# Spreading a side norm over more groups of a feed-forward, moving transposes a part ahead, and four copies a layer to VectorE

## The chip, the cores and the metric

The kernel runs on one core of a Trainium2 chip. The time is the device time of one execution in microseconds (us), as the median of several runs. The engines are TensorE (PE for its matmuls, PEld for its weight loads), VectorE (DVE), ScalarE (ACT), GpSimd (POOL) and the sync engine (SP), whose queue issues the loads of weights.

## The reference

Two layers of a decoder, on 256 tokens of width 1024 and a memory of 256 rows:

```python
mem_n = layer_norm(mem, mem_ln_g, mem_ln_b)
for l in range(DEPTH):                       # DEPTH = 2
    h = layer_norm(ALPHA * x + 0.5 * swiglu(x, ffn1_w_gu, ffn1_w_down), ln_g[0], ln_b[0])
    (dn_q, dn_k, dn_v, dn_b, dn_a, dn_z, sw_q, sw_k, sw_v, xa_q, gates) = split(h @ w_in)
    o_dn = deltanet_branch(...)              # gated delta rule
    o_sw = sliding_window_attention(...)     # 8 heads, window 128, with sinks
    o_xa = memory_cross_attention(xa_q, mem_n, w_mem_kv)
    merged = sum over n of sigmoid(gates[n]) * (branch[n] @ w_branch[n])
    h = layer_norm(ALPHA * h + merged @ w_out, ln_g[1], ln_b[1])
    x = layer_norm(ALPHA * h + 0.5 * swiglu(h, ffn2_w_gu, ffn2_w_down), ln_g[2], ln_b[2])
```

Everything is float32. The norm of the memory (`mem_n`) is computed once and used in both layers.

## The kernel before, in words

**Three matmuls for one product.** Each float32 operand is split into a rounded high half and the rest. `split` (lines 120 and 121) does it: a cast on ScalarE for the high half, then a subtraction on VectorE for the low one. `mm3` multiplies high by high, high by low and low by high. In the profile both instructions of every split, and so those of the weights, stand under line 121, and all matmuls under line 130.

**The stream of weights.** The weights lie in one long stream in the order of use. `unit` (line 104) takes the next 128x1024 block of 512 KB: a load on SP's queue into one of three `raw` buffers (line 115), a cast into one of five `whi` buffers on ScalarE, a subtraction into one of five `wlo` buffers on VectorE. A `raw` buffer can be loaded again when its subtraction is done. Engines and queues run their instructions in the order in which the planner wrote them; the instructions of `unit` are given a priority 300 places ahead of their place in the program (`AHEAD`). `load` (line 76) is for all other loads; those keep the program's order among themselves and share SP's queue with the weights.

**A feed-forward** (`Ffn`) has 11 groups of 256 gate and 256 up columns. A group takes 4 units; per unit TensorE does 2 rows of k for two row blocks of 128 tokens, 12 matmuls of 512 columns. The two banks of a group (of four `acc` banks in PSUM that go round) are read by `out` (line 338): SiLU on ScalarE (line 344), a product on VectorE (line 345) into a tile `t`, a 32x32 transpose on VectorE (line 348), four DMAs on POOL's queue to memory (`tr`, line 354) and one back (`pt`, line 355). `settle` splits what comes back into the high and low halves of the hidden tile. `rest` (line 366) does groups 1 to 10 and then the down projection, 22 units of one k each, into four banks: the first two units are run for row block 0 and then for row block 1, the others for both blocks in turn. So the down projection needs the banks of groups 9 and 10 right behind group 10.

**Side work between groups.** `rest` takes a table `mid`: behind `out` of group i it calls the steps 2i and 2i+1, and what these put on VectorE is queued behind the last product of that group. In layer 0 the table holds the norm of the memory (`memory_T`, line 429) and some loads: step 5 loads small parameters (`small`), 7 and 9 the two row blocks of the stream (`xres`), 8 loads the memory as rows (`vecs`), 10 is `rows_`, 13 loads the transposed memory (`halves_`), 15 and 17 are `half(0)` and `half(1)`, 19 is `keep`.

- `rows_` (line 453) takes mean and variance of each row with bn_stats (459, 460), then the reciprocal root by `rsqrt` (254 to 261), 11 small VectorE instructions, once for each row block; a VectorE transpose (465), four POOL DMAs to memory (467) and one back (469) that spreads means and roots over all partitions, into the tile `gB`.
- `half(q)` (line 476) subtracts the mean (479) and multiplies by the root (480) on 128x1024 of the transposed memory, scales and shifts on ScalarE (483), and splits the result.
- `keep` writes the four halves to memory (441, POOL's queue) for layer 1, which reads them back.

The transposed memory goes into the same two buffers (`pp`) as its rows, so its loads wait for the statistics.

**The mixers** (`mixers`, line 500) keep TensorE's order as written (`pinned`). `weave` runs a generator of matmul parts and calls extra steps behind the part with a given number. Attention weights are turned on TensorE into PSUM (`at`, two banks) by `x_turn` and `w_turn`, and copied out by ScalarE (lines 687 and 741), one copy for each block of 128 keys (`kb`). The values of the window branch go into tiles `oS` (tags u10 and u11), those of the memory branch into `oX` (u6 and u7), whose last reader is `branch(0, oX)`.

The last branch, `branch(2, oT)` (line 960), has four parts of 12 matmuls: row block 0 columns 0 and 1, row block 1 columns 0 and 1. Behind each part VectorE multiplies by the gate (973) and adds to the merged stream `mg` (976). `merge_turn(tb, q)` (line 1011) transposes 128x512 of `mg` on TensorE (line 133) and splits it into `mgT`, the operand of the output projection. `merge_turn(0, 0)` stands behind part 3, `(0, 1)` behind part 4, and `(1, 0)` and `(1, 1)` in `between`, that is after the first two units of the output projection for row block 0. Those two units read only the columns that `merge_turn(0, 0)` makes.

## Time and profile before

| what | before |
|---|---|
| time, median of 3 runs | 1291.05 us (1289.76 to 1291.07) |
| time of the profiled execution | 1291.24 us |
| its span, first to last instruction | 1289.5 us |
| PE busy | 1264.1 us, 98% of the span |
| DVE busy | 855.4 us, 66% |
| ACT busy | 661.3 us, 51% |
| POOL busy | 199.8 us, 15% |
| DMA | 263.50 MB moved, 204 GB/s in the mean |
| granted TensorE clock, mean | 0.995 |

A row of the timeline gives the start and duration in us, the engine, the line, the operation, what it writes and reads, and in brackets how long the engine had been idle before it and what ended that. A row of the groups has the count, the busy us and the mean duration in ns, then the idle us. A row of the waits says which instruction waited for which, with the total us, how often, and the longest. A row of the stage view has a stretch, then for each engine its busy us and instructions, the granted TensorE clock as a share of full speed, and the DMA traffic. TensorE's instructions are pipelined, so a row's duration is longer than the step to the next one.

### The profile page before, as it was taken

The page shows a single profiled execution, that of the slowest core. Times are in us where ns is not written, and L with a number is a line of the kernel's source. Part 1 is how long each engine was busy: PE and PEld are TensorE (multiplying, and loading weights), DVE is VectorE, ACT ScalarE, POOL GpSimd, SP SyncE. Part 2 cuts the span into 40 slices and gives each one's busy share as a digit, 9 for nine tenths or more (in the row PEclk, how much of TensorE's full clock was granted, in tenths as well). Part 3 has the DMA queues.
Part 4 walks back from the last instruction along what each step waited for, and adds up shares of the span by engine and source line. Part 5 has one row for each costly group of instructions (what it writes and reads, how often), then busy time and mean ns, then how long its engine had stood idle before and what let it go on. Part 6 is the DMA issues. An engine that isn't in the chain of part 4 may idle for free.

```text
span 1289.5 us, 18743 instructions
## 1 busy us (share of the span) xinstructions
PE 1264.1 (98%) x6944; PEld 1075.7 (83%) x6944; DVE 855.4 (66%) x1273; ACT 661.3 (51%) x979; POOL 199.8 (15%) x361
## 2 busy tenths in 40 slices
PE   8999899999999999999999999999999999999997
PEld 6887688999878788888888888899988787888886
DVE  5676557797556786665576665758867378666555
ACT  5545444666574545444445444446556554454441
POOL 1232100102411002221012220000023100022200
PEclk9999899999999999999999999999999999999999
DMA  8887774654543648887768777656454256487762
GB/s 271 303 277 255 247 239 125 219 169 136 155 154 122 203 138 272 246 244 229 245 211 262 245 242 213 198 167 209 165 151 146 98 178 231 139 262 241 243 217 107
DMA packets 78075, 263.50 MB, mean 204 GB/s; under 512 B 11968, under 2 KB 13120, under 8 KB 77984
## 3 DMA queue, kind: packets, MB, share of 16 engines
q1 hardware_dynamic: 66320, 232.53, 56.0%
q0 software_dynamic: 11664, 29.77, 8.1%
q8 instruction: 54, 0.88, 0.3%
q14 instruction: 37, 0.30, 0.1%
HBM read 247.45 MB, written 14.81 MB: 203 GB/s over the span
## 4 chain that ended last, share of the span: by engine, by line
PE 75%; DMA 10%; DVE 7%; ACT 4%; issue 3%; POOL 0%; SPq 0%; DVEq 0%; ACTq 0%; POOLq 0%
PE acc L130 65%; DMA raw<-in_wst_dram 9%; PE at L130 3%; PE sm L130 3%; DVE wlo L121 3%; ACT whi L121 2%; PE sm L133 1%; PE acc L326 1%; PE acc L323 1%; PE acc L324 1%; DMA tr<-t 1%; DVE h L286 1%; DVE bnst L272 1%; DVE h L404 1%; DVE u L121 1%
## 5 line engine op out<-in xcount | busy, mean ns | idle before, releaser
L121 DVE TENSOR_TENSOR wlo<-raw,whi 128x1024 fp32r<-128x1024 f32 (+2 forms) x403 | 484.9, 1209 | 329.3 <-ACT whi L121 328.0
L121 ACT CAST whi<-raw 128x1024 fp32r<-128x1024 f32 (+2 forms) x403 | 414.1, 1033 | 444.4 <-PE acc L130 234.7
L130 PE MATMUL acc<-whi,hT 128*128 128x512 f32 (+1 forms) x1824 | 563.6, 387 | 5.0 <-ACT whi L121 5.0
L130 PEld LDWEIGHTS acc<-whi,hT 128*128 128x128 f32 x1824 | 341.3, 188 | 72.9 <-ACT whi L121 5.0
L130 PE MATMUL acc<-wlo,hT 128*128 128x512 f32 (+1 forms) x912 | 351.3, 385 | 0.0
L130 PE MATMUL acc<-whi,u 128*128 128x512 f32 x784 | 252.2, 395 | 6.6 <-DVE t L345 6.6
L130 PEld LDWEIGHTS acc<-wlo,hT 128*128 128x128 f32 x912 | 171.9, 189 | 32.9 <-DVE wlo L121 0.7
L130 PEld LDWEIGHTS acc<-whi,u 128*128 128x128 f32 x784 | 148.4, 189 | 39.9 <-DVE t L345 5.5
L130 PE MATMUL acc<-wlo,u 128*128 128x512 f32 x392 | 153.9, 393 | 0.0
L354 POOL DMA_DIRECT2D tr<-t x176 | 96.2, 553 | 353.3 <-DVE t L348 337.0
L130 PE MATMUL acc<-hT,whi 128*128 128x256 f32 x672 | 122.3, 284 | 0.0
L130 PEld LDWEIGHTS acc<-hT,whi 128*128 128x128 f32 x672 | 104.7, 192 | 0.0
L130 PE MATMUL acc<-hT,wlo 128*128 128x256 f32 x336 | 95.1, 283 | 0.0
L130 PEld LDWEIGHTS acc<-wlo,u 128*128 128x128 f32 x392 | 74.3, 190 | 14.9
L130 PEld LDWEIGHTS acc<-hT,wlo 128*128 128x128 f32 x336 | 64.4, 192 | 0.0
L355 POOL DMA_DIRECT2D pt<-tr x44 | 25.0, 568 | 182.7 <-DMA tr<-t 124.5
L344 ACT ACTIVATE t<-acc 128x256 f32<-128x256 f32 x88 | 32.8, 378 | 23.0 <-PE acc L130 23.0
L345 DVE TENSOR_TENSOR t<-t,acc 128x256 f32<-128x256 f32 x88 | 36.2, 416 | 6.7 <-ACT t L344 4.4
L121 DVE TENSOR_TENSOR u<-pt,u 128x512 fp32r<-128x512 f32 x44 | 29.0, 659 | 10.3 <-ACT u L121 10.3
L529 DVE SCALAR_TENSOR_TENSOR t<-acc,cw,t 128x255 f32<-128x255 f32 (+2 forms) x72 | 34.4, 478 | 0.9
L130 PE MATMUL acc<-whi,w 128*128 128x512 f32 x96 | 31.7, 401 | 2.5 <-DVE w L121 2.5
L121 ACT CAST u<-pt 128x512 fp32r<-128x512 f32 x44 | 26.9, 612 | 12.5 <-DMA pt<-tr 12.5
(248 smaller groups left out, 1188.0 us busy)
## 6 DMA issues: line engine op xcount, KB each, us to landing
raw<-in_wst_dram SPq DMA_DIRECT2D x409, 512.0 KB, 4.3
tr<-t POOLq DMA_DIRECT2D x176, 64.0 KB, 3.8
pt<-tr POOLq DMA_DIRECT2D x44, 256.0 KB, 4.6
raw<-in_wst_dram SPq DMA_DIRECT2D x16, 324.0 KB, 2.8
gB<-in_lnp_dram SPq DMA_DIRECT2D x6, 512.0 KB, 6.4
bB<-in_lnp_dram SPq DMA_DIRECT2D x6, 512.0 KB, 5.8
mdr<-w POOLq DMA_DIRECT2D x4, 512.0 KB, 6.5
w<-dr POOLq DMA_DIRECT2D x4, 512.0 KB, 11.0
```

What stands on the lines that cost most here:

```text
L121: return nc.scalar.copy(hi, src).ins, nc.vector.tensor_tensor(lo, src, hi.bitcast(F32), op=ALU.subtract).ins
L130: return pe(nc.tensor.matmul(*a, **k))
L133: return pe(nc.tensor.transpose(*a))
L272: nc.vector.bn_stats(st[:, done // n, :], y[:, done:done + n])
L286: nc.vector.scalar_tensor_tensor(y[:, cc], y[:, cc], mv[:, 0:1], gB[:, cc], op0=ALU.subtract, op1=ALU.mult)
L323: nc.tensor.matmul(ps, hT[0][:, k, ts], hi[:, c], start=k == 0, stop=False)
L324: nc.tensor.matmul(ps, hT[0][:, k, ts], lo[:, c], start=False, stop=False)
L344: act = nc.scalar.activation(t[:, :, tb, :], g, AF.Silu).ins
L345: ins = nc.vector.tensor_tensor(t[:, :, tb, :], t[:, :, tb, :], u, op=ALU.mult).ins
L354: nc.gpsimd.dma_start(d[:, :, q].rearrange("b c x -> c b x"), z[32 * q:32 * q + 32].rearrange("c (b x) -> c b x", b=4))
L355: nc.gpsimd.dma_start(y, d.rearrange("b c q x -> (b c) (q x)"))
L529: nc.vector.scalar_tensor_tensor(yc[:, j, d:], b[:, j, :S - d], w[:, t:t + 1], yc[:, j, d:], op0=ALU.mult, op1=ALU.add)
```

## The change

The statistics of the memory become a function for one row block, `sums(tb)`, which is called for block 0 behind group 3 and for block 1 in `rows_`; one `rsqrt` then works on both columns. `half` becomes `quarter`, on 128x512. The table in layer 0 is new: loading the memory stands behind group 2 (step 4 instead of 8), `sums(0)` behind 3, `rows_` behind 4 (was 5), loading the transposed memory behind 5 (was 6), the quarters behind 6, 7, 8 and 9 (the halves were behind 7 and 8), `keep` behind 10 (was 9). The small parameters go behind group 6 (was 2) and the two blocks of the stream behind 7 and 8 (were 3 and 4). The copies of turned weights for the second block of keys go to VectorE; these are four a layer, two of `x_turn` and two of `w_turn`. The window branch's values go into tiles u6 and u7. In the last branch `merge_turn(0, 0)` stands behind part 2, `(0, 1)` behind part 3, `(1, 0)` behind part 4, and only `(1, 1)` stays in `between`.

```diff
+        def sums(tb):
+            mv = T(p3, [P, 2], "bnmv")
+            st = T(p3, [P, 4, 6], "bnst")[:, :2, :]
+            for j in range(2):
+                nc.vector.bn_stats(st[:, j, :], got["m"][tb][:, j * 512:j * 512 + 512])
+            nc.vector.bn_aggr(mv, st)
+            nc.vector.tensor_copy(got["st"][:, 0, tb:tb + 1], mv[:, 0:1])
+            nc.vector.tensor_scalar(got["st"][:, 0, 4 + tb:5 + tb], mv[:, 1:2], LN_EPS, None, ALU.add)
+
         def rows_():
-            for tb in range(2):
...
-                rsqrt(got["st"][:, 0, 2 + tb:3 + tb], mv[:, 1:2], T(p3, [P, 1], "rst"))
+            sums(1)
+            rsqrt(got["st"][:, 0, 2:4], got["st"][:, 0, 4:6], T(p3, [P, 2], "mrt"))
...
-        def half(q):
-            m = got["m"][q]
-            mean, rs = (got["row"][:, c:c + S].unsqueeze(1).to_broadcast([P, 4, S]) for c in (0, S))
+        def quarter(n):
+            q, js = n // 2, slice(n % 2 * 2, n % 2 * 2 + 2)
+            m = got["m"][q][:, js]
+            mean, rs = (got["row"][:, c:c + S].unsqueeze(1).to_broadcast([P, 2, S]) for c in (0, S))
             nc.vector.tensor_tensor(m, m, mean, op=ALU.subtract)
             nc.vector.tensor_tensor(m, m, rs, op=ALU.mult)
-            for j in range(4):
-                g, b = (got["gb"][:, n, 4 * q + j:4 * q + j + 1] for n in range(2))
+            for j in range(2):
+                g, b = (got["gb"][:, i, 2 * n + j:2 * n + j + 1] for i in range(2))
                 nc.scalar.activation(m[:, j], m[:, j], AF.Identity, bias=b, scale=g)
-            split(mT[q], mT[2 + q], m)
+            split(mT[q][:, js], mT[2 + q][:, js], m)
-        return {13: again} if l else {8: vecs, 10: rows_, 13: halves_, 15: lambda: half(0), 17: lambda: half(1), 19: keep}
+        return {13: again} if l else {4: vecs, 6: lambda: sums(0), 8: rows_, 11: halves_, 12: lambda: quarter(0), 14: lambda: quarter(1), 16: lambda: quarter(2), 18: lambda: quarter(3), 20: keep}
...
-                nc.scalar.copy(pT[:, kb], ps)
+                (nc.vector.tensor_copy if kb else nc.scalar.copy)(pT[:, kb], ps)
...
-                nc.scalar.copy(wpT[tb][kb][:, :, 2 * hh:2 * hh + 2, :].rearrange(...), ps.rearrange(...))
+                (nc.vector.tensor_copy if kb else nc.scalar.copy)(wpT[tb][kb][:, :, 2 * hh:2 * hh + 2, :].rearrange(...), ps.rearrange(...))
...
-                oS.extend(T(pu, [P, 4, S], tag, F32R) for tag in ("u10", "u11"))
+                oS.extend(T(pu, [P, 4, S], tag, F32R) for tag in ("u6", "u7"))
...
         weave(branch(2, oT), {
-            3: [lambda: merge_turn(0, 0)],
-            4: [lambda: merge_turn(0, 1)]})
+            2: [lambda: merge_turn(0, 0)],
+            3: [lambda: merge_turn(0, 1)],
+            4: [lambda: merge_turn(1, 0)]})
         def between(tb):
             if tb == 0:
-                for q in range(2):
-                    merge_turn(1, q)
+                merge_turn(1, 1)
                 pinned[0] = False
...
-            mid.update({5: small, 7: lambda: xres(0), 9: lambda: xres(1)})
+            mid.update({13: small, 15: lambda: xres(0), 17: lambda: xres(1)})
```

More of the change, by code (lines that the diff above doesn't have):

```diff
@@ L451, in vecs @@
                 load(got["m"][tb], mem[tb * P:(tb + 1) * P, :])
-        def rows_():
-            for tb in range(2):
-                mv = T(p3, [P, 2], "bnmv")
-                st = T(p3, [P, 4, 6], "bnst")[:, :2, :]
-                for j in range(2):
-                    nc.vector.bn_stats(st[:, j, :], got["m"][tb][:, j * 512:j * 512 + 512])
-                nc.vector.bn_aggr(mv, st)
-                nc.vector.tensor_copy(got["st"][:, 0, tb:tb + 1], mv[:, 0:1])
-                nc.vector.tensor_scalar(mv[:, 1:2], mv[:, 1:2], LN_EPS, None, ALU.add)
-                rsqrt(got["st"][:, 0, 2 + tb:3 + tb], mv[:, 1:2], T(p3, [P, 1], "rst"))
+        def sums(tb):
[6 more added lines that the diff above has]
+            nc.vector.tensor_scalar(got["st"][:, 0, 4 + tb:5 + tb], mv[:, 1:2], LN_EPS, None, ALU.add)
+        def rows_():
+            sums(1)
+            rsqrt(got["st"][:, 0, 2:4], got["st"][:, 0, 4:6], T(p3, [P, 2], "mrt"))
             d = T(pd, [4, P], "ms")
@@ L740, in w_turn @@
                     transpose(ps[:, h, :], wpr[tb, hh][:, h, kb * P:(kb + 1) * P], ident)
-                nc.scalar.copy(wpT[tb][kb][:, :, 2 * hh:2 * hh + 2, :].rearrange("p v i q -> p i v q"), ps.rearrange("p (i v) q -> p i v q", v=2))
+                (nc.vector.tensor_copy if kb else nc.scalar.copy)(wpT[tb][kb][:, :, 2 * hh:2 * hh + 2, :].rearrange("p v i q -> p i v q"), ps.rearrange("p (i v) q -> p i v q", v=2))
         def w_values(tb):
             if not oS:
-                oS.extend(T(pu, [P, 4, S], tag, F32R) for tag in ("u10", "u11"))
+                oS.extend(T(pu, [P, 4, S], tag, F32R) for tag in ("u6", "u7"))
             ts = slice(tb * P, (tb + 1) * P)
```

## The prediction

> **What bounds the kernel now.** I read the page first, then who TensorE waited for, then the timelines round the longest of those waits.

> ```profile
> span 1289.5 us, 18743 instructions
> ...
> PE 1264.1 (98%) x6944; PEld 1075.7 (83%) x6944; DVE 855.4 (66%) x1273; ACT 661.3 (51%) x979; POOL 199.8 (15%) x361
> ```

> TensorE has work for 1264.1 of 1289.5 us. Nothing in the change removes a matmul or a transpose, so all it can win is inside the 25.4 us in which PE is idle, and whatever PE loses while its clock is low. All waits of PE over 0.15 us:

> ```profile
> PE acc L130 <- DVE t L345: 6.6, 4, 3.5
> PE acc L130 <- ACT whi L121: 5.0, 1, 5.0
> PE acc L130 <- DVE w L121: 2.5, 2, 1.3
> PE sm L133 <- DVE h L287: 2.0, 5, 0.7
> PE at L133 <- ACT pt L741: 1.1, 2, 0.6
> ```

> Columns are total us, times, longest. The 5.0 is the first weight at the start and the 2.0 lies in the norms of the stream; the change touches neither. It aims at the other three: 6.6 + 2.5 + 1.1 = 10.2 us. The 6.6 is one place, the step from the last group of the first feed-forward to its down projection:

> ```profile
> 127.28 0.39 PE L130 MATMUL acc<-whi,hT 128*128 128x512 f32 x1
> 129.36 0.47 PE L130 MATMUL acc<-whi,u 128*128 128x512 f32 x1 [1.69 <-DVE t L345]
> ...
> 130.83 0.47 PE L130 MATMUL acc<-whi,u 128*128 128x512 f32 x1 [0.54 <-DVE t L345]
> ...
> 132.04 0.62 PE L130 MATMUL acc<-whi,u 128*128 128x512 f32 x2
> ...
> 132.72 0.39 PE L130 MATMUL acc<-whi,u 128*128 128x512 f32 x1
> 136.66 0.79 PE L130 MATMUL acc<-whi,u 128*128 128x512 f32 x1 [3.54 <-DVE t L345]
> 137.25 0.63 PE L130 MATMUL acc<-wlo,u 128*128 128x512 f32 x1
> ...
> 139.13 0.79 PE L130 MATMUL acc<-whi,u 128*128 128x512 f32 x1 [0.83 <-DVE t L345]
> ```

> Three matmuls took 0.68 us (132.04 to 132.72), 0.227 each, and group 10 ended at 127.28 + 0.23 = 127.5. The down projection writes four PSUM banks, and each is free only when L345 (the product of gate and up on VectorE) has read it for group 9 or 10. After the gaps of 1.69 and 0.54 us that pace is whole (the 0.68 comes behind them); after the one of 3.54 a single step takes 0.59 us (136.66 to 137.25). The stage view says why (busy us and instructions of PE, PEld, DVE, ACT and POOL, then the granted clock, 0.87 to 0.50):

> ```profile
> 135.00:137.00 2.00, 0.34 (x1) 0.34 (x2) 1.56 (x2) 0.85 (x3) 0.00 (x0) 0.87 1.00 385
> 137.00:139.00 2.00, 1.30 (x3) 0.48 (x2) 1.48 (x2) 1.29 (x3) 0.00 (x0) 0.50 0.74 285
> 139.00:141.00 2.00, 1.86 (x4) 1.49 (x5) 1.36 (x3) 0.00 (x0) 1.46 (x3) 0.50 0.48 166
> 141.00:143.00 2.00, 2.00 (x6) 1.60 (x5) 0.00 (x0) 0.00 (x0) 1.29 (x3) 0.50 0.98 373
> ```

> Busy time at half clock is 0.34 + 1.30 + 1.86 + 2.00 = 5.5 us, half of it lost: 2.75. The place costs 6.6 + 2.75 = 9.35 us.

> Why was L345 late? VectorE runs in order, and between the products stand the low halves of weights (wlo) still on their way (first VectorE's timeline, then one row of ScalarE's; columns are start, us, engine, line):

> ```profile
> 97.71 0.41 DVE L345 TENSOR_TENSOR t<-t,acc 128x256 f32<-128x256 f32 x1
> ...
> 100.81 0.41 DVE L345 TENSOR_TENSOR t<-t,acc 128x256 f32<-128x256 f32 x1
> ...
> 104.48 1.23 DVE L479 TENSOR_TENSOR pp<-pp,gB 128x1024 f32<-128x1024 f32 x1 [3.26 <-DMA gB<-ms]
> ...
> 135.04 1.23 DVE L121 TENSOR_TENSOR wlo<-raw,whi 128x1024 fp32r<-128x1024 f32 x1 [1.91 <-ACT whi L121]
> 136.19 0.41 DVE L345 TENSOR_TENSOR t<-t,acc 128x256 f32<-128x256 f32 x1
> ...
> 138.67 0.41 DVE L345 TENSOR_TENSOR t<-t,acc 128x256 f32<-128x256 f32 x1
> ```

> ```profile
> 133.97 1.04 ACT L121 CAST whi<-raw 128x1024 fp32r<-128x1024 f32 x1 [3.59 <-DMA raw<-in_wst_dram]
> ```

> Group 10's product at 136.19 stood behind the low half at 135.04, that behind a cast at 133.97, and that waited for its weights. The supply is a ring: a weight load needs one of three raw buffers, freed by a low half, so every us that VectorE loses delays a later load. The memory's norm is such a loss: its first big instruction held VectorE idle for 3.26 us at 104.48, waiting for the broadcast row, with low halves queued behind it.

> A group is 4 units of 12 matmuls, 48 x 0.227 = 10.9 us, so group 7 ended at 127.5 - 3 x 10.9 = 94.8. Its products came 2.9 and 6.0 us after that end; group 10's 8.7 and 11.2. That difference is what the norm cost the supply.

> **The change part by part.** *The norm.* Its work, from VectorE's groups in this stretch (busy us, mean ns) and its timeline:

> ```profile
> L121 DVE TENSOR_TENSOR u<-pt,u 128x512 fp32r<-128x512 f32 x7 | 4.6, 658 | 0.0
> ...
> L479 DVE TENSOR_TENSOR pp<-pp,gB 128x1024 f32<-128x1024 f32 x2 | 2.4, 1222 | 3.3 <-DMA gB<-ms 3.3
> ...
> L259 DVE SCALAR_TENSOR_TENSOR rst<-mst 128x1 f32<-128x1 f32 x6 | 0.9, 153 | 0.0
> ```

> ```profile
> 68.91 0.41 DVE L345 TENSOR_TENSOR t<-t,acc 128x256 f32<-128x256 f32 x1
> ...
> 91.93 0.17 DVE L465 STREAM_TRANSPOSE mst<-mst 128x32 f32<-128x32 f32 x1
> ```

> One reciprocal root for both row blocks instead of two removes 11 tiny instructions, 11 x 0.153 = 1.7 us. Six instructions of 1024 columns become twelve of 512: 6 x (2 x 0.658 - 1.222) = 0.6 us more. VectorE wins 1.1 us. ScalarE's scale-and-shift count is unchanged; its two casts become four smaller ones. So the amount hardly changes; the place does. [...]

> The row is asked for after group 4 instead of 5. Group 4's second product was at 68.91, so the statistics can start at 69.3; they have one block left and one root. Before, they ran from behind group 5 (ended 73.0, its product 6.0 later by group 7's delay: 79.0) to the transpose at 91.93, 12.9 us, and the row arrived 12.55 us after that, at 104.48. Half of 12.9 gives a transpose at 75.8; with 2 us for the head that isn't halved, 78. The row then lands at 88.3 to 90.5. The first quarter stands behind group 6's second product: group 6 ended at 83.9, plus group 7's delay of 6.0 that is 89.9. The 3.26 us wait goes, or shrinks to 0.6. What is late next is again a low half, by as much as the ring lacks without the norm.

> I therefore give group 10 the delays of group 7. Bank three is then free at 127.5 + 2.9 + 0.41 = 130.8; PE comes to it after 12 matmuls, at 130.2, and waits 0.6. After three matmuls (131.5) it needs bank four, free at 127.5 + 6.0 + 0.41 = 133.9: 2.4 more. Stall 3.0 instead of 6.6: **3.6 us won**. Bounds: nothing left (6.6 won) and 4.7 lost (second rival).

> Does the clock still halve? A gap of 1.69 did not do it and one of 3.54 did; the new longest, 2.4, is nearer to the first, so I count no loss, bounds 0 and 2.75: **2.75 us won**. [...]

> *What moves with it.* The same six 512 KB loads (memory twice, its transpose twice, the stream's two blocks) pass the weights on SP's queue, the memory first and the stream last; in a stretch where loads set the pace, order costs nothing, and the stream's blocks are needed only behind the down projection. SP's second copy of the memory waits until statistics have freed its buffer, with weight loads behind it:

> ```profile
> SPq L78 <- DVE bnst L459: 0.9, 1, 0.9
> ```

> I take the same 0.9 us as now (bounds 0 and 1.8, twice it); those loads end in the ring too. The four writes of the normed memory on POOL's queue now stand after group 10's transposes, not before them; they are hidden under the down projection, and they delay by their own issue only the last bounce, which is needed at its end.

> *The second copies.* Now, on ScalarE, on TensorE and on VectorE, then VectorE's groups by shape and all its waits for a cast of weights:

> ```profile
> 377.11 0.59 ACT L741 COPY pt<-at 128x512 f32<-128x512 f32 x1
> ```

> ```profile
> 377.75 0.66 PE L133 MATMUL at<-cs,pp 128*128 128x128 f32 x4 [0.56 <-ACT pt L741]
> ```

> ```profile
> 377.25 1.23 DVE L121 TENSOR_TENSOR wlo<-raw,whi 128x1024 fp32r<-128x1024 f32 x1 [3.52 <-ACT whi L121]
> ```

> ```profile
> L121 DVE TENSOR_TENSOR u<-at,u 128x512 fp32r<-128x512 f32 x8 | 5.5, 689 | 2.0 <-ACT u L121 1.6
> ```

> ```profile
> DVE wlo L121 <- ACT whi L121: 328.0, 260, 3.8
> ```

> PE waits 0.56 us for the copy at 377.11, a second one. VectorE reads such a bank in 0.69 us (the 689) and is idle for 3.52 us before 377.25; in the whole trace it waited 260 times for a cast, 1.26 us each. So eight copies hide in idle time: **1.1 us won** in two layers. If the order puts them behind that low half (377.25 + 1.23 + 0.69 = 379.2 against 377.7), PE waits 1.5 more, 3.0 in two layers.

> *The transposes a part ahead.* VectorE's rows, then TensorE's:

> ```profile
> 434.77 0.69 DVE L976 TENSOR_TENSOR u<-u,gt 128x512 f32<-128x512 f32 x1
> ...
> 442.13 0.68 DVE L121 TENSOR_TENSOR w<-sm,w 128x512 fp32r<-128x512 f32 x1
> ```

> ```profile
> 437.36 0.60 PE L133 MATMUL sm<-cs,u 128*128 128x128 f32 x4
> ```

> The first transposes (437.36, behind part three) are split only at 442.13, and PE waits 1.25 for that, in each layer. A part earlier is 437.36 - 12 x 0.227 = 434.6, but the first part's sum is written only at 434.77 + 0.69 = 435.46: a new wait of 0.86. Net 1.25 - 0.86 = 0.4 a layer, **0.8 us won**. Bounds: 2.5 won if that sum moves up, 1.7 lost if the split stays late as well. The window branch's buffers move to a pair free since the branch before: nothing.

> Sum: 3.6 + 2.75 + 1.1 + 0.8 = 8.25 us. The profiled execution took 1291.24 (its span of 1289.5 and 1.7 round it), which gives 1283.0; the median of the runs is 1291.05, 0.2 less, so 1282.8.

> **The rivals.** *The supply fills up.* Without the long wait the ring may run as far ahead as it does in the other three feed-forwards: all 4 of the waits for L345 above lie in this one place. Then 6.6 + 2.75 + 1.1 + 2.5 = 12.95: 1278.1. For it: only this place has the wait; against: already group 7 was 6.0 late.

> *Pieces in front of the last products (slower).* Two quarters now follow groups 8 and 9. If the last stands ahead of group 10's products, these come 3 x 0.66 = 2.0 us later, and a low half more (one unit, 12 x 0.227 = 2.7) makes 4.7. It decides once the first product comes after 136.19. With the other wins of 1.9 the time is 1291.05 + 4.7 - 1.9 = 1293.9. For it: 1.23 us pieces held the queue before; against: the pieces are half as long.

> *The row is late again.* If the first quarter meets a row as late as 104.48 was, all 9.35 stay and only 1.9 is won: 1289.2. This is also the case that the spreading does not do what it says.

> *The clock halves all the same* after a gap of 2.4: 1282.8 + 2.75 = 1285.6. Neither gap above excludes it. [...]

> **How the numbers follow.** Forecast 0.42, supply full 0.20, clock 0.10, row late 0.17, pieces in front 0.11. About 0.2% (2.6 us) is what a measurement of this kernel can tell: faster below 1288.5 is 0.42 + 0.20 + 0.10 = 0.72, within it 0.17, slower 0.11. The range runs from the full supply, less 0.6, to the late row plus 1 us for its open terms: 1277.5 to 1290.2; it leaves out the slower case and some edges.

> **What would show it.** Right: the wait of PE on L345 near 3 us with no gap over 3.4 and the clock at 1.00 round 137; no idle of VectorE for gB over 1 us; no wait on L741; a new one of PE on L976's sum near 0.86, and none on the split. Wrong: group 10's products still over 8 us behind its end, a new wait on a copy by VectorE, or PE waiting for weights within groups 5 to 9.

## The result, and the profile after

The changed kernel takes 1282.9 us in the median (1280.74 to 1285.74, 6 runs), the kernel before 1291.01 us (1289.76 to 1292.11, 6 runs) on the same chip. The ratio is 0.9941, with a 95% interval of 0.9926 to 0.9956: 8.1 us less. The forecast was 1282.8 us, from 1277.5 to 1290.2. The time is right; whether the reasons are is another question.

The profiled execution took 1282.78 us. The first lines of its page, and all waits of TensorE over 0.15 us:

```profile
span 1280.7 us, 18740 instructions
...
PE 1261.9 (99%) x6944; PEld 1075.1 (84%) x6944; DVE 859.7 (67%) x1276; ACT 658.8 (51%) x973; POOL 200.3 (16%) x361
```

```profile
PE acc L130 <- ACT whi L121: 5.0, 1, 5.0
PE acc L130 <- DVE t L345: 2.1, 2, 1.6
PE sm L133 <- DVE u L981: 2.1, 3, 1.0
PE sm L133 <- DVE h L287: 1.5, 4, 0.5
```

The span fell by 8.8 us. PE's idle time (span less busy) went from 25.4 to 18.8 us, by 6.6, and its busy time by 2.2. The wait on L345 fell from 6.6 to 2.1, and the copy's wait of 1.1 is gone. The wait of 2.5 for the split of the turned stream is gone too, but one of 2.1 for the sum (L976 before, L981 now) stands in its place.

The place behind group 10, on TensorE's timeline, and VectorE's timeline at the same time:

```profile
132.24 0.50 PE L130 MATMUL acc<-whi,u 128*128 128x512 f32 x1 [1.58 <-DVE t L345]
...
133.70 0.69 PE L130 MATMUL acc<-whi,u 128*128 128x512 f32 x1 [0.51 <-DVE t L345]
```

```profile
129.67 0.69 DVE L121 TENSOR_TENSOR w<-pp,w 128x512 fp32r<-128x512 f32 x1 [0.42 <-ACT w L121]
130.63 1.23 DVE L121 TENSOR_TENSOR wlo<-raw,whi 128x1024 fp32r<-128x1024 f32 x1 [0.26 <-ACT whi L121]
131.77 0.41 DVE L345 TENSOR_TENSOR t<-t,acc 128x256 f32<-128x256 f32 x1
132.10 1.22 DVE L121 TENSOR_TENSOR wlo<-raw,whi 128x1024 fp32r<-128x1024 f32 x1
133.24 0.41 DVE L345 TENSOR_TENSOR t<-t,acc 128x256 f32<-128x256 f32 x1
```

The order on VectorE is still the old one: each product behind a low half. But the low halves behind which the products stand hardly wait for their casts any more: 0.26 us and nothing, where before it was 1.91 and 0.92. The products of group 10 start at 131.77 and 133.24, where before they started at 136.19 and 138.67.

The norm's row, on VectorE's timeline: the transpose of the statistics, then the first quarter.

```profile
76.29 0.21 DVE L468 STREAM_TRANSPOSE mst<-mst 128x32 f32<-128x32 f32 x1
...
91.87 0.69 DVE L483 TENSOR_TENSOR pp<-pp,gB 128x512 f32<-128x512 f32 x1 [1.74 <-DMA gB<-ms]
```

VectorE still waits for the row, but 1.74 us instead of 3.26. And the clock still halves. Four stretches of 3.41 us in the stage view (busy us and instructions of PE, PEld, DVE, ACT and POOL, then the granted clock):

```profile
127.03:130.44 3.41, 3.41 (x16) 2.65 (x15) 1.92 (x2) 3.38 (x5) 0.51 (x1) 1.00 0.67 203
130.44:133.85 3.41, 1.32 (x5) 0.63 (x5) 3.02 (x4) 2.16 (x5) 1.16 (x3) 1.00 0.87 292
133.85:137.26 3.41, 3.41 (x9) 2.64 (x10) 0.00 (x0) 0.23 (x1) 0.00 (x0) 0.50 0.98 366
137.26:140.67 3.41, 3.41 (x17) 2.78 (x15) 2.99 (x5) 2.65 (x4) 1.38 (x3) 1.00 0.55 202
```

In the third stretch the clock is 0.50 and PE starts 9 matmuls instead of 16 or 17: 3.41 / 2 = 1.7 us are lost there.

### The profile page after: what moved, and what is told of

Read it like the earlier page. It is cut to its first block, busy times and chain, and to the rows that moved or that the text cites. A ratio compares the mean times of both kernels' runs of the same rounds, so it can differ in the third digit from the quotient of the medians.

```text
span 1280.7 us, 18740 instructions
## 1 busy us (share of the span) xinstructions
PE 1261.9 (99%) x6944; PEld 1075.1 (84%) x6944; DVE 859.7 (67%) x1276; ACT 658.8 (51%) x973; POOL 200.3 (16%) x361
## 4 chain that ended last, share of the span: by engine, by line
PE 80%; DMA 9%; DVE 6%; ACT 3%; issue 1%; POOL 0%; SPq 0%; DVEq 0%; ACTq 0%; POOLq 0%
PE acc L130 70%; DMA raw<-in_wst_dram 7%; PE sm L130 3%; PE at L130 3%; DVE wlo L121 2%; ACT whi L121 2%; PE sm L133 1%; PE acc L326 1%; DMA tr<-t 1%; PE at L133 1%; DVE u L121 1%; PE acc L323 1%; PE acc L324 1%; DMA ms<-mst 1%; DVE h L287 0%
## 5 line engine op out<-in xcount | busy, mean ns | idle before, releaser
L121 DVE TENSOR_TENSOR wlo<-raw,whi 128x1024 fp32r<-128x1024 f32 (+2 forms) x403 | 484.0, 1208 | 305.6 <-ACT whi L121 303.0
L121 ACT CAST whi<-raw 128x1024 fp32r<-128x1024 f32 (+2 forms) x403 | 414.5, 1033 | 443.2 <-PE acc L130 202.9
L130 PE MATMUL acc<-whi,hT 128*128 128x512 f32 (+1 forms) x1824 | 563.4, 387 | 5.0 <-ACT whi L121 5.0
L130 PEld LDWEIGHTS acc<-whi,hT 128*128 128x128 f32 x1824 | 341.4, 189 | 73.0 <-ACT whi L121 5.0
L130 PE MATMUL acc<-wlo,hT 128*128 128x512 f32 (+1 forms) x912 | 351.0, 385 | 0.0
L130 PE MATMUL acc<-whi,u 128*128 128x512 f32 x784 | 251.1, 394 | 2.1 <-DVE t L345 2.1
L130 PEld LDWEIGHTS acc<-wlo,hT 128*128 128x128 f32 x912 | 171.8, 188 | 32.8 <-DVE wlo L121 0.4
L130 PEld LDWEIGHTS acc<-whi,u 128*128 128x128 f32 x784 | 147.9, 189 | 33.9 <-DVE t L345 2.9
L130 PE MATMUL acc<-wlo,u 128*128 128x512 f32 x392 | 153.5, 391 | 0.0
L130 PE MATMUL acc<-hT,whi 128*128 128x256 f32 x672 | 122.2, 284 | 0.0
L130 PEld LDWEIGHTS acc<-hT,whi 128*128 128x128 f32 x672 | 104.6, 192 | 0.0
L130 PE MATMUL acc<-hT,wlo 128*128 128x256 f32 x336 | 95.0, 283 | 0.0
L130 PEld LDWEIGHTS acc<-wlo,u 128*128 128x128 f32 x392 | 74.0, 189 | 14.9
L130 PEld LDWEIGHTS acc<-hT,wlo 128*128 128x128 f32 x336 | 64.3, 191 | 0.0
L345 DVE TENSOR_TENSOR t<-t,acc 128x256 f32<-128x256 f32 x88 | 36.3, 416 | 6.1 <-ACT t L344 4.0
L121 DVE TENSOR_TENSOR u<-pt,u 128x512 fp32r<-128x512 f32 x44 | 29.1, 662 | 11.5 <-ACT u L121 11.5
L121 ACT CAST u<-pt 128x512 fp32r<-128x512 f32 x44 | 27.0, 613 | 12.4 <-DMA pt<-tr 12.4
L348 DVE STREAM_TRANSPOSE t<-t 128x512 f32<-128x512 f32 x44 | 31.2, 709 | 1.0
```

Of the source, the lines that this page charges most:

```text
L121: return nc.scalar.copy(hi, src).ins, nc.vector.tensor_tensor(lo, src, hi.bitcast(F32), op=ALU.subtract).ins
L130: return pe(nc.tensor.matmul(*a, **k))
L345: ins = nc.vector.tensor_tensor(t[:, :, tb, :], t[:, :, tb, :], u, op=ALU.mult).ins
L348: ins = nc.vector.transpose(z, t.rearrange("p j t x -> p (j t x)")).ins
```

## The experiments

**My theory:** the early row is nearly all of the gain, by way of the ring of weights; the copies win what they hide; the turns are close to nothing. **Rivals:** the cutting into quarters does it, or the new order of the loads; the order of VectorE's queue alone makes the stall, and the supply has no part in it; the turns win what the split's wait was. All ratios are to the kernel before on the same chip. The kernel before itself ranged from 1287.8 to 1295.7 us in 29 runs, and the intervals below reach at least 0.1% to each side, so one microsecond can't be told from the time; where the times don't decide, the waits do.

### The three parts, each alone

The first kernel has the new norm (`sums`, the one root, `quarter`, the new table, the moved loads) on the kernel before, and nothing else:

```diff
-        return {13: again} if l else {8: vecs, 10: rows_, ...
+        return {13: again} if l else {4: vecs, 6: lambda: sums(0), 8: rows_, 11: halves_, 12: lambda: quarter(0), ...
```

> The kernel before with the norm's part of the change alone (statistics, early row, quarters, moved loads). Theory: the norm is nearly all of the gain, because it takes the place between group 10 and the down projection from 6.6 us idle and 2.75 us lost at half clock to 2.1 and 1.7, as in the changed kernel: 5.5 us, so 1285.5 us, with the wait on the split of the merged stream (2.5) and on the copy L741 (1.1) still there. Rival: the three parts share the gain and the norm alone wins 3 us or less.

Measured: 1282.33 us, ratio 0.9933 (0.9917 to 0.9948). All of the gain is here, 8.8 us against the 5.5 expected. Some of PE's waits in its profile:

```profile
PE acc L130 <- DVE w L121: 3.0, 2, 1.6
PE at L133 <- ACT pt L745: 1.1, 2, 0.6
...
PE acc L130 <- DVE t L345: 0.2, 1, 0.2
```

The waits of the other two parts stand as before; the wait on L345 is down to 0.2, and the clock isn't halved at that place. VectorE's busy time is 854.6 us against 855.4, so the norm itself costs it about as much as ever; the gain doesn't come from work saved.

The second has only the copies on VectorE:

```diff
-                nc.scalar.copy(pT[:, kb], ps)
+                (nc.vector.tensor_copy if kb else nc.scalar.copy)(pT[:, kb], ps)
```

> The kernel before with the second copies on VectorE alone. Theory: the waits of PE on L741 (1.1 us in all) go and nothing takes their place: 1289.9 us. Rival: the copies stand behind a low half that waits for its cast, and PE waits up to 3 us for a copy by VectorE: 1291 to 1294.

Measured: 1289.89 us, ratio 0.9991 (0.998 to 1.0002). The copy's wait is gone and none on a copy by VectorE has come. A gain of 1.1 us fits, but so does none.

The third has only the turns a part ahead:

```diff
-            3: [lambda: merge_turn(0, 0)],
-            4: [lambda: merge_turn(0, 1)]})
+            2: [lambda: merge_turn(0, 0)],
+            3: [lambda: merge_turn(0, 1)],
+            4: [lambda: merge_turn(1, 0)]})
```

> The kernel before with the transposes a part ahead alone. Theory: the wait on the split (2.5 us in all) goes and one on the first part's sum comes, 0.9 in each layer: net 0.7 won, 1290.3 us. Rival: the sum's wait is as long as the split's, nothing won: 1291.

Measured: 1291.59 us, ratio 1.0004 (0.9991 to 1.0018). The split's wait is gone, and this row of PE's waits has come:

```profile
PE sm L133 <- DVE u L976: 2.4, 3, 1.1
```

2.4 us came for the 2.5 that went: the turns win nothing that can be measured.

### Where the norm's gain comes from

Three kernels on the kernel before. The first asks for the row early, with the one root and the moved loads, but keeps two halves in place of four quarters:

```diff
+        return {13: again} if l else {4: vecs, 6: lambda: sums(0), 8: rows_, 11: halves_, 15: lambda: half(0), 17: lambda: half(1), 19: keep}
```

> The kernel before with the statistics and the broadcast row as early as in the change and the loads moved as there, but the normalisation still in two halves behind groups 7 and 8. Theory: what cost most was VectorE idle for the row with low halves behind it; here the row lands ten us before the first half, so nearly all of the norm's gain is there, 1282 to 1284.5 us, and the profile has no idle of VectorE for gB. Rival: the size of the pieces is what matters, and halves keep the stall: 1288 to 1291.

Measured: 1288.23 us, ratio 0.9968 (0.9955 to 0.998). There is no wait of VectorE for the row any more, and yet PE waits 4.8 us on L345 and the clock halves for 6.83 us. By its time this is the rival's side.

The second has the quarters and the one root, but the row at its old place:

```diff
+        return {13: again} if l else {8: vecs, 10: lambda: (sums(0), rows_()), 13: halves_, 14: lambda: quarter(0), ..., 17: lambda: quarter(3), 19: keep}
```

> The kernel before with quarters instead of halves and one root for both blocks, but all of it behind the same groups as before (row behind 5, two quarters behind 7 and two behind 8), loads as before. Theory: the row still comes late and holds VectorE for about 3 us, group 10's products stay 8 us or more behind its end, and little is won: 1288 to 1291 us. Rival: smaller pieces are what wins: 1282 to 1285.

Measured: 1289.17 us, ratio 0.9972 (0.9959 to 0.9985). This is the time that the theory gave, but not its reason: the wait for the row is 1.7 us and not 3, though the row is asked for no earlier. That on L345 is 4.7, and the clock halves for 6.83 us.

The third only moves the loads of the small parameters and of the stream:

```diff
-            mid.update({5: small, 7: lambda: xres(0), 9: lambda: xres(1)})
+            mid.update({12: small, 14: lambda: xres(0), 16: lambda: xres(1)})
```

> The kernel before with only the loads of the stream's two blocks and of the small parameters moved behind groups 6 to 8. Theory: in a ring that sets the pace their order is worth nothing: 1290 to 1292 us. Rival: weights come sooner early on, the cushion lasts, and part of the norm's gain is in this: 1284 to 1288.

Measured: 1292.09 us, ratio 0.9996 (0.9985 to 1.0007): nothing. So the early row with halves wins 0.32%, the quarters with the late row 0.28%, and the whole norm 0.67%. My theory that the row's wait is nearly everything falls: the early place and the small pieces have about equal shares, which together make most of the 0.67. But neither run is purely one part. One root less comes with both, so what it is worth is counted in both, and it was not tried by itself; and with the quarters the wait for the row fell too, from 3.3 to 1.7 us. By which step small pieces win so much isn't shown.

### The order of the queue

Here the kernel before has the splits of the fourth and fifth weights of each down projection queued behind the last SiLU and the last product of group 10, so that SiLU and product no longer stand behind these splits:

```diff
-            projA(..., post, along=self.settle, ends=ends)
+            projA(..., post, behind=(self.silu, self.last), held=(3, 4), along=self.settle, ends=ends)
```

> The kernel before, norm untouched; in every feed-forward the splits of the fourth and fifth unit of the down projection are queued behind the last group's SiLU on ScalarE and product on VectorE. Theory: the stall is the place of the products in VectorE's queue, not a lack of weights: the waits on the product go, 9.35 us less at most 2 us of waits for the first weights of the down projection, 1282 to 1284 us. Rival: the ring is simply empty there, and the same wait comes back as PE waiting for a low or high half: 1287 to 1291 us.

Measured: 1289.01 us, ratio 0.9978 (0.9965 to 0.999). PE's wait on L345 falls from 6.6 to 1.3 us and the clock stays whole there; some 8 us of the place are gone, but only 2.8 of them show in the time. Most of the rest has moved. One row of its waits of PE (two lines further down in the code than before), the low half on VectorE right ahead of the norm's first instruction, and the stretch in which the wait lies and the next one:

```profile
PE sm L135 <- DVE h L289: 3.4, 3, 2.7
```

```profile
184.47 1.23 DVE L123 TENSOR_TENSOR wlo<-raw,whi 128x1024 fp32r<-128x1024 f32 x1 [1.92 <-ACT whi L123]
```

```profile
191.07:194.48 3.41, 1.28 (x11) 1.08 (x10) 3.41 (x12) 1.99 (x2) 0.00 (x0) 1.00 0.02 6
194.48:197.89 3.41, 2.82 (x13) 2.83 (x14) 3.02 (x4) 1.17 (x2) 0.00 (x0) 0.50 0.03 10
```

PE now waits 2.7 us in the norm of the stream behind the down projection, and the clock halves there instead. In that stretch VectorE is never idle; it runs the norm, which began behind a low half that had waited 1.92 us for its cast. So the order of the queue makes the stall on L345, but taking that stall away gave back only a third of it. That late weights are the reason is read from these rows; no run tests it.

The same hold on the changed kernel, where the weights are earlier:

> The changed kernel, and with it the hold tried on the kernel before: the splits of the fourth and fifth unit of each down projection stand behind the last SiLU and product of group 10. Theory (the ring of weights is now ahead by some 4 us when group 10 ends, so the hold costs nothing later): PE's wait on L345 goes from 2.1 to under 0.5 us, the clock isn't halved round 135 us, no new wait for weights in the down projection; 1282.9 less 2.1 + 1.7 = 1279.1 us, ratio near 0.991. Rival (what the hold takes from the place comes back later, as it did on the kernel before, 2 us of the 9.4 left): waits of PE for whi or wlo near 143 to 145 us or for a norm's rows at 195 us, 1282 to 1283 us, ratio near 0.9935.

Measured: 1281.57 us, ratio 0.9916 (0.9903 to 0.9929). The interval overlaps that of the changed kernel in the same call (below: 0.991 to 0.9953), so a gain isn't shown. The wait on L345 (L347 in this code) is still 1.9 us, which the theory excluded. Its rows, on PE, VectorE and ScalarE:

```profile
133.01 0.50 PE L132 MATMUL acc<-whi,u 128*128 128x512 f32 x1 [1.88 <-DVE t L347]
```

```profile
130.29 1.22 DVE L123 TENSOR_TENSOR wlo<-raw,whi 128x1024 fp32r<-128x1024 f32 x1 [1.75 <-ACT whi L123]
131.94 0.69 DVE L123 TENSOR_TENSOR w<-pp,w 128x512 fp32r<-128x512 f32 x1 [0.42 <-ACT w L123]
132.54 0.75 DVE L347 TENSOR_TENSOR t<-t,acc 128x256 f32<-128x256 f32 x2
```

```profile
129.21 1.05 ACT L123 CAST whi<-raw 128x1024 fp32r<-128x1024 f32 x1 [3.58 <-DMA raw<-in_wst_dram]
130.16 1.09 ACT L489 ACTIVATE pp<-pp,mgb 128x256 f32<-128x256 f32 x2
131.28 0.62 ACT L123 CAST w<-pp 128x512 fp32r<-128x512 f32 x1
131.81 0.65 ACT L346 ACTIVATE t<-acc 128x256 f32<-128x256 f32 x2
```

The hold did what it says; the products now stand together, with no low half between. But ahead of them, on ScalarE, stand a cast that waited 3.58 us for its weights, then the last quarter's scale, shift and cast, and only then SiLU (L346). Here the late load holds up the products by ScalarE's queue, and the last quarter stands behind it and ahead of them.

### The turns again, and the copies

The changed kernel, with the split of the output projection's third weight queued behind the first part's sum:

```diff
-... ("u8", "u9"))], 2, post, led=between, ends=ends)
+... ("u8", "u9"))], 2, post, behind=sums_[-4], held=(2,), led=between, ends=ends)
```

> The changed kernel, with the split of the output projection's third unit queued on VectorE behind the first part's sum (L981), so that this sum no longer stands behind a low half that waits for its cast. Theory: the waits of PE on the sum, 0.85 and 1.02 us in the changed kernel, go: 1.9 us less than the changed kernel, 1281.0 us. Rival: the sum is earlier but the low half behind it is then late for the output projection, or the split of the first transposes waits instead: no gain, 1282.9.

Measured: 1284.91 us, ratio 0.9935 (0.9921 to 0.9949), which is the changed kernel's. The wait on the sum falls from 2.1 to 1.4 us, and those in the norms of the stream (L287) are 3.1, not 1.5. But the second profile of the changed kernel (below) has 2.7 and 4.7, so the rise can't be laid to the edit, and a gain isn't shown.

The norm and the copies without the turns (and with the window branch's buffers where they were):

> The norm and the copies without the turns a part ahead. Theory (the turns are worth nothing, the copies 1.1 us, and the two add): as the changed kernel, 1282 to 1283 us, ratio near 0.993; PE's wait for the split of the turned stream is there again with 2.5 to 3.0 us, none on the add, none on a copy. Rival (the turns win the 0.8 us forecast): 1283.7 us. The two lie within what five rounds can tell; the waits decide.

Measured: 1283.1 us, ratio 0.9927 (0.9911 to 0.9943). The split's wait is back with 3.2 us, the sum's gone, and no copy is waited for. With the turns or without, the times can't be told apart.

These with the hold:

> The norm, the copies and the hold, without the turns. Theory: if the hold wins on the changed kernel, it wins here as much, 1279 to 1280 us. Rival: as without the hold, 1282 to 1283 us.

Measured: 1282.74 us, ratio 0.9922 (0.9909 to 0.9935): as without the hold, the rival's side.

And the changed kernel once more:

> The changed kernel once more, unedited, to see in a second profile which of its waits and which half clock are its own. Theory (the wait on L345 depends on when single loads land and scatters): the wait is between 0 and 4 us and need not be the 2.1 of the first profile; the clock is halved round 135 us where the idle time of PE within 3.4 us is over half, and not where it is less. Rival (the wait is fixed by the order of the queue): 2.1 us again within 0.3, and the half clock again. Time 1282.9 us, ratio 0.993 to 0.9955, either way.

Measured: 1283.36 us, ratio 0.9931 (0.991 to 0.9953). All of PE's waits over 0.15 us in this second profile:

```profile
PE acc L130 <- ACT whi L121: 4.9, 1, 4.9
PE sm L133 <- DVE h L287: 4.7, 6, 1.7
PE sm L133 <- DVE u L981: 2.7, 2, 1.5
PE acc L130 <- DVE t L345: 0.5, 1, 0.5
```

The wait on L345 is 0.5 here, not 2.1, and the clock isn't halved at that place; but the norms of the stream wait 4.7 instead of 1.5. The row isn't waited for either. The program is the same: the 2.1 is one execution's number. The same cast of weights on ScalarE, the last one ahead of the last quarter's scale and shift, in the first profile and then in the second:

```profile
126.95 1.05 ACT L121 CAST whi<-raw 128x1024 fp32r<-128x1024 f32 x1 [3.15 <-DMA raw<-in_wst_dram]
```

```profile
124.77 1.05 ACT L121 CAST whi<-raw 128x1024 fp32r<-128x1024 f32 x1 [1.95 <-DMA raw<-in_wst_dram]
```

Its weights landed 2.2 us sooner in the second; why isn't shown. No version tried is measurably faster than the changed kernel.

### When the clock halves

From the time that the clock first comes up until the last matmul, each low stretch of the clock lasts 3.41 us (the changed kernel), or two or three times that (6.83 in the kernel before, 10.24 with the turns alone). From the low stretch behind group 10 to the next one at the end, full clock lasts 1140.0 us in the profile before as in the one after, which is 334 times 3.413 within 0.2 us. So I count time in stretches of 3.41 us here. The stage view of six profiles, cut at those stretches, shows in each which share of a stretch PE was busy and what clock the next had. In the kernel before, first the stretch with its gap of 1.69, then the two with that of 3.54 and what followed:

```profile
126.23:129.64 3.41, 1.72 (x8) 1.15 (x7) 3.12 (x4) 3.41 (x7) 1.44 (x3) 1.00 0.75 245
129.64:133.05 3.41, 2.87 (x12) 1.80 (x10) 3.38 (x5) 0.74 (x1) 1.41 (x4) 1.00 0.97 325
133.05:136.46 3.41, 0.06 (x1) 0.00 (x0) 1.50 (x3) 1.34 (x3) 0.88 (x2) 1.00 1.04 398
136.47:139.88 3.41, 2.39 (x5) 1.48 (x6) 2.45 (x5) 1.82 (x3) 0.57 (x1) 0.50 0.69 264
139.88:143.29 3.41, 3.41 (x10) 2.64 (x9) 0.52 (x1) 0.00 (x0) 2.17 (x4) 0.50 0.80 291
```

Busy for 1.72 of 3.41 us, 50%: the clock stayed. Busy for 0.06: it halved. Then the kernel in which only the loads are moved (stayed, at 1.73), and the hold on the changed kernel:

```profile
127.20:130.61 3.41, 1.73 (x7) 0.81 (x5) 3.41 (x5) 3.41 (x6) 1.09 (x2) 1.00 0.82 215
130.61:134.02 3.41, 2.33 (x9) 1.61 (x9) 2.71 (x4) 0.00 (x0) 2.08 (x4) 1.00 0.92 326
```

```profile
131.41:134.82 3.41, 1.81 (x8) 1.50 (x9) 2.96 (x6) 3.41 (x6) 2.16 (x4) 1.00 0.71 199
134.82:138.24 3.42, 3.42 (x17) 2.83 (x16) 2.17 (x4) 0.81 (x3) 1.71 (x4) 1.00 1.04 380
```

Last the norm, copies and hold without the turns, its gap and its stretches:

```profile
132.21 0.50 PE L132 MATMUL acc<-whi,u 128*128 128x512 f32 x1 [1.86 <-DVE t L347]
```

```profile
130.08:133.49 3.41, 1.55 (x8) 1.06 (x7) 2.70 (x6) 2.60 (x6) 0.57 (x1) 1.00 0.98 282
133.49:136.90 3.41, 3.41 (x10) 2.64 (x9) 2.67 (x3) 1.44 (x2) 2.78 (x6) 0.50 0.78 251
```

A gap of 1.88 us (133.01, above) left the clock whole and one of 1.86 halved it. The difference is where the gap lay. The first reaches over the edge of a stretch at 131.41, so that PE was busy for 1.81 us (53%) of the stretch; the second lies within one, which leaves 1.55 us (45%). By the same count the changed kernel's 1.32 (39%) halved it, and so did the 1.28 of the hold on the kernel before. These agree with a limit between 45% and 50% busy in a stretch. A stretch far from this place, in the kernel with the third weight's split queued behind the sum, brings the two sides closer:

```profile
455.31:458.72 3.41, 1.58 (x15) 1.41 (x14) 3.34 (x9) 0.51 (x2) 0.00 (x0) 1.00 0.26 106
458.72:462.14 3.42, 3.42 (x29) 3.28 (x28) 2.76 (x8) 1.15 (x2) 0.00 (x0) 1.00 0.02 5
```

Busy for 1.58 us (46%), so idle for over half, and the clock stayed. Of the stretches at full clock counted so, those with PE busy for 0.06, 0.12 (only the loads moved, at 134.03), 0.79 (the turns alone, at 131.74), 1.28, 1.32, 1.48 (norm and copies, at 131.64) and 1.55 us were followed by half clock; those with 1.58, 1.72, 1.73 and 1.81 were not. In the whole profiles of the kernel before and of the changed kernel, from the clock's first rise to the last matmul, one more has PE busy for under 2.1 us: the one in which the matmuls of the kernel before end (1279.93, 1.46 us), with half clock behind it. The limit is read from these cases, and no run was made to set the gap on purpose.

## Why the prediction was right in its time, and where it was wrong

- **The stall on L345: right in kind, its size too large.** Forecast 3.0 us left, in gaps of 0.6 and 2.4; measured 2.1 in the first profile (1.58 and 0.51) and 0.5 in the second. The cause was argued rightly as the lateness of the low halves. What failed is the premise that group 10 would get group 7's delays of 2.9 and 6.0 us: its products came 4.0 and 5.5 us behind its end (127.8) in the first profile, and 2.2 and 3.6 in the second. The wait differed by 1.6 us between two executions of one program.
- **Pieces in front: the rival's condition came about, its size did not.** The last quarter's split (129.67, above) stands ahead of both products of group 10, but the first of them came at 131.77, not after 136.19. With the queue held, the last quarter is part of what is left. In the norm, copies and hold without the turns, its scale on ScalarE, with SiLU behind it, waits for its own multiply on VectorE (L486):

```profile
129.35 1.09 ACT L489 ACTIVATE pp<-pp,mgb 128x256 f32<-128x256 f32 x2 [1.10 <-DVE pp L486]
```

No run takes the last quarter away from there, so what it costs is open.

- **The clock: this step failed.** "The new longest, 2.4, is nearer to the first, so I count no loss." The longest gap was 1.58, shorter than the 1.69 which had left the clock whole, and the clock halved all the same, for 1.7 of the 2.75 us counted as won. (The loss before was nearer to 2.9: PE was busy for 2.39 and 3.41 us of the two stretches at half clock, which reach to 143.29.) I had judged single gaps; what counts, by the stretches above, is how busy PE was in 3.41 us, and here two gaps, 1.58 + 0.51, fell into one. The rival that it halves all the same happened in the first profile, without its price of 2.75, and not in the second. No run shows the 3.4 us that the last line of the prediction sets as the limit for a gap: longest gaps of 1.58 and 1.86 us halved the clock, where PE was busy for 39% and 45% of a stretch.
- **The row: the place was right, its landing late.** The transpose came at 76.29, as forecast (75.8 to 78). The row landed at 91.87, not 88.3 to 90.5, because it took 15.6 us on its way instead of 12.55, and the wait was 1.74 us, not at most 0.6; in the second profile there was none. The prediction took the row for the cause of the supply's loss, and that step failed: the stall doesn't follow the row's wait. In the norm alone VectorE waits 2.1 us for the row and PE 0.2 on L345; with the early row and halves VectorE waits nothing for it and PE 4.8. The early row with halves and the quarters with the late row each win about half. I had put the change of 1024 to 512 columns down as 0.6 us lost; it is among what wins, though what it wins without the single root isn't shown.
- **VectorE's work for the norm:** forecast 1.1 us less, measured 0.8 in the norm alone (855.4 to 854.6). The kernel that only moves loads has the same instructions on VectorE as the kernel before and 853.6 us, so 0.8 can't be told from nothing.
- **SP's queue:** the loads behind the statistics wait 2.2 us in the profile after, for 1.5 before (the 0.9 that I counted, and 0.6 for the second load, which I left out); my upper bound was 1.8. Nothing of it is seen in the time.
- **The copies: right by the waits**, 1.1 us gone and none in its place; the time alone can't show it.
- **The turns: the wait was seen, its price was not.** Forecast 0.86 us a layer on the sum, measured 0.85 (below) and 1.02 with 0.19 more, 2.1 in all, and 2.4 to 2.7 in other profiles. So 0.4 us net or less, not 0.8; the times of the runs with and without the turns can't be told apart. The rows, TensorE's and then VectorE's:

```profile
428.25 0.63 PE L133 MATMUL sm<-cs,u 128*128 128x128 f32 x4 [0.85 <-DVE u L981]
```

```profile
426.27 1.22 DVE L121 TENSOR_TENSOR u<-raw,u 128x1024 fp32r<-128x1024 f32 x1 [0.80 <-ACT u L121]
427.42 0.68 DVE L981 TENSOR_TENSOR u<-u,gt 128x512 f32<-128x512 f32 x1
```

The sum stands behind a low half that waited for its cast: the same pattern as behind group 10.

- **The sum.** From 1291.24 to 1282.78 us in the profiled executions is 8.46 us, forecast 8.25. Measured in the terms of the forecast: stall 4.5 (3.6), clock 2.9 - 1.7 = 1.2 (2.75), copies 1.1 (1.1), turns 0.4 (0.8): 7.2. The norms of the stream, which I had left alone, give 0.5; 0.8 us I can't put to a row. So errors of +0.9, -1.55 and -0.4 and 1.3 us from elsewhere made a right total: that it fell within 0.1 us of the median is chance. That it is the norm's work which costs time behind group 10 is not chance: the norm alone has all of the gain, and with it the wait and the half clock at that place shrink or go. That it does so by way of late weights is read from the rows.

## What to carry to other kernels

Where the supply sets the pace, side work on the supplying engine is priced by where it stands and how large its pieces are, not by its busy time: starting it earlier and cutting it finer each won about 0.3% here (each together with one root less) with hardly any work saved. A wait that you take off the path by reordering a queue can return at the next consumer, as most of it did here, so try the reorder by itself and look for the new wait before you count it. Judge a clock risk by how busy TensorE is in each whole stretch, two short gaps together (of 3.41 us here, 1.55 busy or less was followed by half clock, 1.58 or more was not), and take the wait of one execution as a sample.
